# State-space stage of a streaming encoder: decay of the initial states and sums of squares on VectorE in place of Pool

## The chip, the core and the metric

The kernel runs on one core of a Trainium2 chip. The metric is the device time of one execution in microseconds (us). Five engines work side by side, each through its own instructions in order: TensorE (PE, with its weight loads as PEld), VectorE (DVE), ScalarE (ACT), Pool (GpSimd) and SyncE (SP), which here only starts transfers. TensorE writes into PSUM, in banks of 512 floats per partition; VectorE and ScalarE read them out. An instruction waits on semaphores for what it needs, and everything behind it on its engine waits too.

## The reference

One layer of a hybrid encoder for two groups of requests: a prompt of 1024 frames, and 8 requests of 16 frames with a past (caches of keys and values, of the convolution and of the state). After a modulated norm there is one input projection; branch A is chunked attention, branch B a state-space scan (Mamba-2 SSD); the two are gated, merged and projected. The change lies in branch B:

```python
def step(h, inp):                      # h: state per head, (64, 128)
    x, d, bk, ck = inp
    a_cs = jnp.cumsum(d * ag, axis=1)
    ...
    y_in = jnp.einsum('blsge,bsgep->blgep', cb[..., None] * decay, xdt)
    y_st = jnp.einsum('blgn,bgepn->blgep', ck, h) * jnp.exp(a_cs)[..., None]
    h_new = h * jnp.exp(a_cs[:, -1])[..., None, None] + jnp.einsum(...)
...
y = y * jax.nn.silu(z_ssd)
y = rms_norm(y.reshape(b, s, SSD_GROUPS, 512), ...)
```

For the 8 requests `h` starts from `state_ssm`: each new state is the initial state times its decay, plus a product over the 16 frames. The norm needs the sum of squares of `y` over a group of 512 channels, which are four pairs of heads of 128 channels.

## The kernel before

All 1152 tokens (1024 + 8 x 16) lie along the free axis, channels along the 128 partitions. The projections are float32 products in three parts: weights and activations are split into a high and a low half, and each output of 128 x 384 takes 8 x 3 matmuls (L384, L385, L387, the "dense" matmuls); the split of a weight block is L321 on ScalarE and L322 on VectorE. Outputs collect in PSUM tiles `d` (two banks) and `s` (one); small products use the tiles `g` out of a pool `psg` of four banks. `pg()` hands out a `g` tile, and its next user waits until the old one has been read.

The stages follow each other: attention over 8 units, then the state-space stage (about 860 to 1640 us of the span) over 16 pairs of heads in 4 groups, then the output projections.

In the state-space stage a pair `p` consists of three generators. `dense_gen` issues the dense matmuls of x (evicted by L1066 to L1070, then the convolution L1086 to L1096) and of z (L1255, L1256), and in ten pairs those of a merge gate (evicted by L1187, stored by L1188). `prelude` loads the decays, broadcast over the partitions (L1273, L1277), and the initial states (L1279), and makes the decay matrices (L1285, L1289 on ScalarE, L1291 on VectorE). `main` does the pair's own products:

- transposes of x (L1313), scaled by L1317; halves of the last rows for the requests' states (L1339, L1340) and their masked copies, four per pair, on Pool (L1347)
- the chunk states L1358 (`g` tiles), chained by L1363 and L1367; the last one is stored (L1372)
- the outputs within chunks L1385 (three `g` tiles), the initial states' part L1392, then L1398 on VectorE; the chunk states' part L1405, then L1410 and L1411
- the initial states times their decays, L1418 on Pool, 128 x 1024
- gating with z, L1419 on VectorE; y is stored (L1421), its square made on ScalarE (L1422)
- the requests' state products L1429 into two `g` tiles, two masked copies for each; each tile is added to the decayed states on VectorE (L1438); the result is stored (L1447)
- the squares are added up over the group's four pairs, L1444 on Pool, 128 x 1152 (the first pair's square is the start, so there are twelve additions)

After a group's fourth pair the sums go over the partitions (L766) and through a square root; the next group's transposes and products (L1216, L1222) share the same four banks.

The order of the work is not the order of the text. `run` steps the generators by a clock of estimated nanoseconds: a generator that yields a number has issued so much TensorE work, and `pause(t)` holds it until the clock has gone on by `t`. A scheduler then sorts the instructions by its own estimate of when they can start, so on each engine an instruction can move past others; `late(...)` keeps some in order. After a build the order on every engine is fixed.

Of the kernel before, what the change touches and what calls it, by code (L numbers as in the profile page):

```python
# [10 lines left out]
ALU = mybir.AluOpType  # L11

P = 128
# [3 lines left out]
NB = 8  # L17
# [4 lines left out]
HD = 64  # L22
# [89 lines left out]
def trunk_kernel(ctx: ExitStack, tc: tile.TileContext, h):  # L112
    nc = tc.nc
# [104 lines left out]
    def alloc(lay, tag, cols):  # L218
        if lay is L_Q:
            try:  # L220
                return alloc(L_QR, tag, cols)
            except NoSlot:
                pass
        if lay is L_SSD and tag == "H":
            try:
                return Buf(qarena, qarena.alloc(L_QS, "ada", cols), cols)
            except NoSlot:
                pass
        if lay is L_Q or lay is L_QS:
            return Buf(qarena, qarena.alloc(lay, tag, cols), cols)  # L230
        if lay is L_W3 or lay is L_VT or lay is L_VA:
            return Buf(varena, varena.alloc(lay, tag, cols), cols)
        if lay is L_H or lay is L_W or lay is L_WA or lay is L_QR or lay is L_ST:
            return Buf(rarena, rarena.alloc(lay, tag, cols), cols)
        if (lay is L_SSD or lay is L_HEAD or lay is L_TAIL) and tag == "T" or lay is L_HEAD and tag == "Y":
            if v_open[0]:
                try:
                    return alloc(L_VT, "T", cols)
                except NoSlot:
                    pass  # L240
        return Buf(arena, arena.alloc(lay, tag, cols), cols)
# [250 lines left out]
    sq = [alloc(L_START, "T", NT) for _ in range(2)]  # L492
# [211 lines left out]
    def until(t):  # L704
        while clock[0] < t:
            yield -1.0

    def pause(t):
        yield from until(clock[0] + t)
# [522 lines left out]
    def ssd(p):  # L1232
# [8 lines left out]
        s4 = decs.rearrange("p (b e) -> p b e", e=32)  # L1241
# [53 lines left out]
        def main():  # L1295
            yield from ready(lambda: "z" in st and "cbm" in grp[g] and "t" in dts and st["x"])
            x, tx = st["x"][0]
            z = st["z"]
            res = grp[g]
# [115 lines left out]
            stored(hst)  # L1415

            h4 = h0.ap.rearrange("p (b e d) -> p b e d", e=2, d=HD)
            nc.gpsimd.tensor_tensor(h4, h4, s4[:, :, 2 * p:2 * p + 2].unsqueeze(3).to_broadcast([P, NB, 2, HD]), ALU.mult)  # L1418
            nc.vector.scalar_tensor_tensor(x.ap, x.ap, 0.5, z.ap, ALU.mult, ALU.mult)  # L1419
            yield from pause(1800)  # L1420
            store(y_d[p], x.ap)  # L1421
            nc.scalar.activation(z.ap, x.ap, AF.Square)  # L1422
# [18 lines left out]
            if res["sq"] is None:  # L1441
                res["sq"] = z
            else:
                nc.gpsimd.tensor_tensor(res["sq"].ap, res["sq"].ap, z.ap, ALU.add)  # L1444
                z.free()
            yield from pause(1200)
            store(h["out_hs"][p], h0.ap)  # L1447
# [1 line left out]
            if p % PPG == PPG - 1:  # L1449
# [8 lines left out]
                if p == NPAIR - 1:  # L1458
                    dts["x"].free()

        return dense_gen(), [prelude()], [main()], 0.5


# [285 lines left out]
```

## Time and profile before

| | |
|---|---|
| time, median of 3 runs | 2037.41 us (2037.35 to 2038.08) |
| the profiled execution | 2043.03 us, span 2041.2 us |
| TensorE busy | 2014.5 us, 99% of the span |
| VectorE / ScalarE / Pool busy | 1163.9 / 766.0 / 405.9 us |
| granted TensorE clock, mean | 0.994 |
| TensorE's longest waits | 10.0 us at the start, 4.2 us in the state-space stage |
| L1418 on Pool | 16 times, median 1.91 us |
| L1444 on Pool | 12 times, median 2.67 us |

How to read the lines: the list of waits names who waited for what, with the total in us, the number of times and the longest. The chain gives start, duration and engine of the work that ended last. A timeline row gives start, duration, engine, line, operation, output and inputs, and in brackets the idle time before it and what ended it. A window row gives its bounds and length, then the busy time of PE, PEld, DVE, ACT and POOL with instruction counts, the granted clock (1.00 is full), the share of the DMA engines and GB/s. A row of groups ends with busy time and mean duration, then the idle time before the group. A row of one line gives the shortest, median and longest duration in ns.

### The profile page before, as it was taken

To read this page: it belongs to the slowest core of one execution; us is meant where nothing else is said; L and a number is where in the kernel's file an instruction comes from. 1 tells how busy PE (TensorE), PEld (TensorE's weight loads), DVE (VectorE), ACT (ScalarE), POOL (GpSimd) and SP (SyncE) were. 2 spreads that over 40 slices of the span, in tenths; PEclk is the share of its full clock that TensorE was granted. 3 is DMA by queue.
4 is the path that set the end of the run, shared out by engine and by line. 5 is a ranking of instruction groups with operands and counts; after the bars stand their busy time and mean duration, and the time that the engine had idled before them with its cause. 6 is when DMAs were issued, how large, how long until landed. Compare 5 with 4: busy or idle time off the path is not lost.

```text
span 2041.2 us, 35394 instructions
## 1 busy us (share of the span) xinstructions
PE 2014.5 (99%) x14223; PEld 1879.7 (92%) x14223; DVE 1163.9 (57%) x2424; ACT 766.0 (38%) x1560; POOL 405.9 (20%) x657
## 2 busy tenths in 40 slices
PE   7999999999999999999999999999999999999999
PEld 5888888888888888999999999999999999999999
DVE  6445454554554566456775677557764533777732
ACT  5344443443434444444534444345443311111210
POOL 0123121231212210123332234224323210000000
PEclk9999999999999999999999999999998999999999
DMA  7233232332323232333333433243325663331331
GB/s 311 88 103 104 72 127 76 127 101 95 110 86 127 68 102 84 103 123 120 121 99 111 124 109 121 93 126 128 120 89 191 251 224 103 126 100 54 100 118 62
DMA packets 81371, 239.63 MB, mean 117 GB/s; under 512 B 14316, under 2 KB 15352, under 8 KB 81208
## 3 DMA queue, kind: packets, MB, share of 16 engines
q1 hardware_dynamic: 72248, 208.73, 31.3%
q0 software_dynamic: 8960, 28.65, 3.6%
q8 instruction: 112, 1.84, 0.4%
q14 instruction: 51, 0.42, 0.1%
HBM read 193.39 MB, written 43.95 MB: 116 GB/s over the span
## 4 chain that ended last, share of the span: by engine, by line
PE 96%; DVE 2%; DMA 1%; ACT 1%; issue 0%; SPq 0%; DVEq 0%; ACTq 0%
PE d L384 13%; PE d L387 13%; PE d L385 13%; PE s L384 5%; PE d L440 5%; PE s L385 5%; PE d L438 5%; PE s L387 5%; PE d L439 5%; PE g L969 4%; PE g L908 3%; PE s L939 3%; PE g L1385 2%; PE g L1358 1%; PE g L1405 1%; PE g L1028 1%
## 5 line engine op out<-in xcount | busy, mean ns | idle before, releaser
L384 PE MATMUL d<-rarena 128*128 128x384 f32 x1536 | 527.8, 344 | 1.0 <-ACT rarena L321 1.0
L385 PE MATMUL d<-rarena 128*128 128x384 f32 x1536 | 518.3, 337 | 0.0
L387 PE MATMUL d<-rarena 128*128 128x384 f32 x1536 | 517.5, 337 | 0.2 <-DVE rarena L322 0.2
L384 PEld LDWEIGHTS d<-rarena 128*128 128x128 f32 x1536 | 289.7, 189 | 6.3 <-issue 3.8
L387 PEld LDWEIGHTS d<-rarena 128*128 128x128 f32 x1536 | 289.4, 188 | 3.0 <-issue 2.1
L385 PEld LDWEIGHTS d<-rarena 128*128 128x128 f32 x1536 | 290.0, 189 | 1.8 <-issue 1.5
L321 ACT ACTIVATE rarena<-arena 128x1024 fp32r<-128x1024 f32 x97 | 102.6, 1058 | 301.0 <-PE s L385 188.6
L384 PE MATMUL s<-rarena 128*128 128x384 f32 x624 | 213.6, 342 | 1.3 <-DVE arena L901 1.3
L385 PE MATMUL s<-rarena 128*128 128x384 f32 x624 | 209.7, 336 | 0.0
L387 PE MATMUL s<-rarena 128*128 128x384 f32 x624 | 209.5, 336 | 0.0
L438 PE MATMUL d<-va_att,rarena 128*128 128x384 f32 x576 | 200.1, 347 | 0.3 <-DVE arena L689 0.3
L440 PE MATMUL d<-va_att,rarena 128*128 128x384 f32 x576 | 199.4, 346 | 0.0
L439 PE MATMUL d<-va_att,rarena 128*128 128x384 f32 x576 | 198.0, 344 | 0.0
L322 DVE TENSOR_TENSOR rarena<-arena,rarena 128x1024 fp32r<-128x1024 f32 x97 | 125.9, 1298 | 94.3 <-ACT rarena L321 93.3
L901 DVE CUSTOM_DVE_ANT_0 arena<-s,arena 128x320 f32<-128x320 f32 (+5 forms) x208 | 99.5, 513 | 135.1 <-PE s L939 112.3
L896 ACT ACTIVATE arena<-arena 128x640 f32<-128x640 f32 (+3 forms) x144 | 101.2, 706 | 97.0 <-DVE arena L901 51.8
L384 PEld LDWEIGHTS s<-rarena 128*128 128x128 f32 x624 | 117.8, 189 | 3.4 <-issue 1.6
L385 PEld LDWEIGHTS s<-rarena 128*128 128x128 f32 x624 | 117.9, 189 | 0.4 <-issue 0.4
L387 PEld LDWEIGHTS s<-rarena 128*128 128x128 f32 x624 | 117.6, 188 | 0.0
L440 PEld LDWEIGHTS d<-va_att,rarena 128*128 128x128 f32 x576 | 108.3, 188 | 7.0 <-issue 6.3
L438 PEld LDWEIGHTS d<-va_att,rarena 128*128 128x128 f32 x576 | 108.4, 188 | 6.8 <-issue 5.6
L910 ACT ACTIVATE arena<-g 128x512 f32<-128x512 f32 (+3 forms) x144 | 71.0, 522 | 114.0 <-PE g L908 113.6
(332 smaller groups left out, 3358.7 us busy)
## 6 DMA issues: line engine op xcount, KB each, us to landing
arena<-in_wall_dram SPq DMA_DIRECT2D x88, 512.0 KB, 3.9
arena<-in_kc_dram SPq DMA_DIRECT2D x64, 256.0 KB, 3.0
arena<-in_vc_dram SPq DMA_DIRECT2D x64, 256.0 KB, 2.8
arena<-acs_d SPq DMA_DIRECT2D x20, 576.0 KB, 3.6
gate_d<-arena POOLq DMA_DIRECT2D x48, 192.0 KB, 2.2
y_d<-arena POOLq DMA_DIRECT2D x15, 576.0 KB, 3.4
arena<-y_d SPq DMA_DIRECT2D x15, 576.0 KB
arena<-in_wssd_dram SPq DMA_DIRECT2D x16, 512.0 KB, 3.5
```

Source lines behind the costliest of these rows:

```text
L321: keep(nc.scalar.activation(hi.r[:, c], b.ap, AF.Copy))
L322: keep(nc.vector.tensor_tensor(lo.r[:, c], b.ap, hi.ap[:, c], ALU.subtract))
L384: nc.tensor.matmul(ps, hi.r[:, wc], kh.r[:, tok], start=k == 0, stop=False)
L385: nc.tensor.matmul(ps, hi.r[:, wc], kl.r[:, tok], start=False, stop=False)
L387: nc.tensor.matmul(ps, lo.r[:, wc], kh.r[:, tok], start=False, stop=k == nk - 1)
L438: nc.tensor.matmul(ps, kh.r[:, tok], hi.r[:, wc], start=k == 0, stop=False)
L439: nc.tensor.matmul(ps, kh.r[:, tok], lo.r[:, wc], start=False, stop=False)
L440: nc.tensor.matmul(ps, kl.r[:, tok], hi.r[:, wc], start=False, stop=k == KT - 1)
L896: nc.scalar.activation(p, p, AF.Exp, bias=sm_[:, 4 + e:5 + e], scale=-1.0, accum_out=sm_[:, 6 + e:7 + e])
L901: late(nc.vector.tensor_tensor_reduce(p, ps, bap, -1.0, 3.0e38, ALU.add, ALU.min, least))
L910: nc.scalar.activation(pt.ap[:, j * P:(j + n) * P], ps[:, :n * P], AF.Copy)
L969: nc.tensor.matmul(ps[e * HD:e * HD + HD, :], v.ap[:, vc:vc + HD], pts[e].ap[:, j * P:(j + 1) * P], start=j == 0, stop=j == np_ - 1)
```

## The change

The product of the initial states with their decays goes from Pool to VectorE, and in the generator it stands behind the gating and a pause of 800. The addition of the squares goes from Pool to VectorE in its place. No instruction is added or taken away. All lines from L1418 on carry other numbers in the changed file: the gating is L1418, the product L1420, the store of y L1422, the square L1423, the state products L1430, the state addition L1439, the addition of squares L1445.

```diff
             h4 = h0.ap.rearrange("p (b e d) -> p b e d", e=2, d=HD)
-            nc.gpsimd.tensor_tensor(h4, h4, s4[:, :, 2 * p:2 * p + 2].unsqueeze(3).to_broadcast([P, NB, 2, HD]), ALU.mult)
             nc.vector.scalar_tensor_tensor(x.ap, x.ap, 0.5, z.ap, ALU.mult, ALU.mult)
+            yield from pause(800)
+            nc.vector.tensor_tensor(h4, h4, s4[:, :, 2 * p:2 * p + 2].unsqueeze(3).to_broadcast([P, NB, 2, HD]), ALU.mult)
             yield from pause(1800)
             store(y_d[p], x.ap)
             nc.scalar.activation(z.ap, x.ap, AF.Square)
...
             else:
-                nc.gpsimd.tensor_tensor(res["sq"].ap, res["sq"].ap, z.ap, ALU.add)
+                nc.vector.tensor_tensor(res["sq"].ap, res["sq"].ap, z.ap, ALU.add)
                 z.free()
```

## The prediction

> **What bounds the kernel now.** I read the page first, then the list of TensorE's waits, then the stage in windows, and last the chain and the timelines around the one long wait of the stage that the change touches.
>
> ```profile
> span 2041.2 us, 35394 instructions
> PE 2014.5 (99%) x14223; PEld 1879.7 (92%) x14223; DVE 1163.9 (57%) x2424; ACT 766.0 (38%) x1560; POOL 405.9 (20%) x657
> PE 96%; DVE 2%; DMA 1%; ACT 1%; issue 0%; SPq 0%; DVEq 0%; ACTq 0%
> ```
> ```profile
> PE g L503 <- DMA arena<-in_xT_dram: 10.0, 1, 10.0
> PE g L1385 <- DVE arena L1438: 4.2, 1, 4.2
> PE s L597 <- DVE rarena L584: 3.4, 4, 1.6
> ```
> ```profile
> 804.90:808.30 3.40, 1.82 (x16) 1.18 (x14) 3.40 (x12) 3.40 (x6) 0.92 (x3) 1.00 0.28 54
> 808.35:811.70 3.35, 3.35 (x11) 3.35 (x12) 3.35 (x5) 2.45 (x6) 0.00 (x0) 0.50 0.70 262
> 1532.20:1535.30 3.10, 0.00 (x0) 0.00 (x0) 3.10 (x1) 0.00 (x0) 2.35 (x1) 1.00 1.04 351
> 1535.40:1545.50 10.10, 9.12 (x71) 9.12 (x72) 8.00 (x26) 1.25 (x3) 3.09 (x3) 0.50 0.75 217
> 860.00:1640.00 780.00, 775.12 (x5515) 765.01 (x5514) 500.02 (x793) 328.38 (x654) 234.67 (x315) 0.99 0.39 130
> ```
>
> TensorE is busy 99% of the span and carries 96% of the chain. The change removes no matmul. So VectorE's and Pool's shares decide nothing by themselves: the time can move only where TensorE waits, or where its clock is cut. In the state-space stage (860 to 1640 us) VectorE is busy 500 of 780 us, Pool 235, TensorE 775. What TensorE lacks there is one place, its wait in L1385 for the second state addition L1438, in pair 14 (counted from 0). The chain through it:
>
> ```profile
> 1507.07 0.89 PE g L1358 x8
> 1508.13 0.17 PE s L385
> 1518.85 1.24 issue
> 1523.79 1.27 DVE arena L1291
> 1526.65 1.14 DVE va_ssd L1095
> 1527.78 0.20 DVE va_ssd L1096
> 1529.02 1.34 DVE arena L1419
> 1530.38 1.17 ACT arena L1422
> 1531.56 4.08 DVE rarena L322
> 1535.63 0.61 DVE arena L1438
> 1545.29 0.32 PE d L384
> 1545.83 0.18 PE d L387
> ```
> ```profile
> 1531.05 0.29 PE L1385 MATMUL g<-arena,va_ssd 128*64 128x128 f32 x1 [0.64 <-issue]
> 1531.87 0.27 PE L1385 MATMUL g<-va_ssd 128*64 128x128 f32 x1
> 1536.38 0.45 PE L1385 MATMUL g<-arena,va_ssd 128*64 128x128 f32 x1 [4.23 <-DVE arena L1438]
> ```
> ```profile
> 1531.25 0.73 POOL L1347 TENSOR_TENSOR rarena<-rarena,arena 128x256 fp32r<-128x256 f32 x1
> 1531.95 2.60 POOL L1444 TENSOR_TENSOR arena<-arena 128x1152 f32<-128x1152 f32 x1
> ```
>
> L1385 fills three PSUM tiles out of a pool of four, and its second tile takes the bank of the state product that L1438 adds up. TensorE idles 0.64 + 4.23 = 4.87 us. Then comes a part that a list of waits does not show: from 1535.4 to 1545.5 the granted clock is 0.50 (a 128x384 matmul advances by 0.32 us, afterwards by 0.18), so the 9.12 us of work in that window lose 9.12 / 2 = 4.6 us. This one place costs 4.87 + 4.6 = 9.4 us.
>
> **The change part by part.**
>
> ```profile
> L1418 POOL TENSOR_TENSOR qa_ssd<-qa_ssd,arena x8: 1902/1914/2030, 875.2 to 1540.5; 128x1024 f32<-128x1024 f32 x8
> L1444 POOL TENSOR_TENSOR arena<-arena x6: 2597/2673/2997, 1186.6 to 1622.3; 128x1152 f32<-128x1152 f32 x6
> L322 DVE TENSOR_TENSOR rarena<-arena,rarena x97: 1209/1222/4093, 20.6 to 2013.4; 128x1024 fp32r<-128x1024 f32 x97
> L1291 DVE TENSOR_TENSOR arena<-arena x13: 1345/1351/2474, 1077.7 to 1578.8; 128x1152 f32<-128x1152 f32 x13
> ```
>
> *What leaves Pool and comes to VectorE.* Sixteen products h0 x decay at 1.91 us and twelve additions of squares at 2.67 us leave Pool. No row shows them on VectorE. Its product of the same 1024 columns has a median of 1.22 us (L322), its product of 1152 columns 1.35 us (L1291); between nothing and Pool's own 1.91 and 2.67 I take these, being the same kind of instruction on the same engine. VectorE gains 16 x 1.22 + 12 x 1.35 = 35.7 us over the stage, 2.6 us in a pair with both. Where VectorE is not awaited this costs nothing: TensorE's dense matmuls cover it (between a pair's state products and the next pair's L1358 stand some 110 to 150 of them in most pairs, 19 to 26 us). Where that cover is gone, in pair 14, the 2.6 us are on the path and are in the sum below.
>
> *What VectorE no longer meets.* L322 at 1531.56 takes 4.08 us in place of 1.22. It began while Pool ran L1347, Pool's L1444 followed from 1531.95 to 1534.55, and L322 ended 1.1 us after that. Without L1444 on Pool 2.87 us of it go. [...]
>
> *The pause and the order.* The pause of 800 moves the planner's clock, and with it everything behind. In the built order nothing but that order changed from pair 1 on, and the product stands early, between L1410 and L1411, ahead of the gating (L1419, in the changed file L1418): the pause doesn't hold it back there. What matters is pair 14. In the built order of before 75 dense matmuls stand between the first L1358 of pair 13 and the second L1385 tile of pair 14, in the new one 81, with the same other matmuls. After the bank's last state product, before: 5 of L1358 and one tile of L1385 ahead of its reuse; now 10 dense, 8 of L1358 and that tile (the trace shows each L1358 and L1385 as two records). By row spacings the distance grows from 2.1 to 4.5 us. No other reuse of a bank in the stage is closer than 3.3 us now, and reuses that near stood elsewhere in the old order without a wait.
>
> *TensorE's side of pair 14.* From 1507.07 to the end of the first L1385 tile (1531.87 + 0.27) are 25.1 us, less 0.64 idle 24.4. Six more dense matmuls at 0.174 make 25.5. The second tile adds 0.9, and at 26.4 comes a gate's dense matmul whose bank waits for L1256.
>
> *VectorE's side.* L1438 ended at 1536.24, 29.2 us after 1507.07. In the new order L322 (4.08) and L1095 with L1096 (1.14 + 0.20) stand behind that addition, and the two moved instructions (1.22 + 1.35) before it: 29.2 - 4.08 - 1.34 + 2.57 = 26.3 us. Both L1291 now stand later, behind the gating, so the 1.24 us in which VectorE waited for the first one's exponentials can go too: 25.1 us. Against 25.5 TensorE waits 0 to 0.8 us. Then L322 (1.22) and L1256:
>
> ```profile
> L1256 DVE SCALAR_TENSOR_TENSOR arena<-arena,d 128x384 f32<-128x384 f32 x23 | 12.5, 548 | 3.3 <-ACT arena L1255 3.1
> ```
>
> 26.9 to 28.1 us, against 26.4: 0.5 to 1.7 us of waiting in all. I take 1.1.
>
> *The clock after a short wait.* The first two windows above show 1.58 us without a matmul, and then 3.35 us at clock 0.50: 1.7 us lost, against 4.6 behind the idle 4.23. The nearest case thus says 1.7; but the matmuls around that gap were small ones, here they are dense, so I charge half, 0.85. [...]
>
> *New waits in order.* The addition of squares now waits on VectorE for ScalarE's Square, with the second L1438 queued behind it and TensorE behind that. Square takes 1.17 us from the end of the gating, and two L1291 (2.6 us) stand between: covered in pair 14. On Pool the masked copies (L1347) and the stores of y and of the state move up; SP's loads of h0 wait for those stores and can only come sooner. That is taken as nothing, since TensorE waits for none of them before.
>
> **Sum.** -9.4 + 1.1 + 0.85 = -7.4 us. The profiled execution took 2043.0 us, its span 2041.2 with 1.8 around it; it would become 2035.6. The median of the runs is 2037.4, 5.6 below the profiled one; I carry the same difference over: **2030.0 us**.
>
> **The rivals.** About 0.2% (4.1 us) is what a measurement of this kernel can tell from no change: 2033.3 and 2041.5 are the bounds.
>
> *The same wait again.* TensorE's gate matmul waits for L1256, that for L1255, and that for the store of the pair's y:
>
> ```profile
> ACT arena L1255 <- DMA y_d<-arena: 4.4, 1, 4.4
> 1530.65 0.58 POOL L1421 DMA_DIRECT2D y_d<-arena  x1 [1.51 <-PE g L1358]
> ```
>
> The store issued at 1530.65 let L1255 go at 1536.11, 5.4 us on. In the new order the gating ends some 19.4 us after the first L1358 (23.3 - 2.6 - 1.3 - 1.2 + 1.2), so the store lands at about 25.4 and L1256 ends at 26.4, in time. Were it to land 5 us later, the 4.9 us of waiting and the half clock would be back: 2037.4.
>
> *The wait is smaller without the profiler.* The runs are 5.6 us shorter than the profiled execution; if part of that is this very wait, less is there to win. With half of it gone, 4.7 - 2.0 = 2.7 us: 2034.7. The narrow spread of the runs (0.7 us) speaks neither for nor against.
>
> *Slower: the group boundaries.* At the starts of groups 1 to 3 (pairs 3, 7, 11) transposes and products for the next group share the four banks with the state products. Reuse distances there are 3.7 to 5.1 us, and the built order now puts the addition of squares, waiting in order for Square, right before the evictions:
>
> ```profile
> 1229.45 1.22 DVE L1095 SCALAR_TENSOR_TENSOR arena<-arena 128x1024 f32<-128x1024 f32 x1
> 1232.99 2.85 DVE L322 TENSOR_TENSOR rarena<-arena,rarena 128x1024 fp32r<-128x1024 f32 x1 [0.93 <-ACT rarena L321]
> 1235.76 0.68 DVE L1224 TENSOR_TENSOR arena<-g,arena 128x512 f32<-128x512 f32 x1
> ```
>
> Against it: L322 took 2.85 there and nothing waited, and those 1.6 us of collision go. It decides from the point where the eviction comes later than its reuse: if the moved 2.6 us came on top in full at each boundary with 1.7 us of clock, 3 x 4.3 = 12.9 are lost, and with the 7.4 won the kernel takes 2042.9.
>
> **How the numbers follow.** The forecast has 0.66; its own range runs from 0.5 us of waiting and a full clock (gain 8.9, 2028.5) to a gain of 4.1 (2033.3). The same wait 0.12 and the smaller wait 0.10 fall within 0.2%; the boundaries 0.12. The range for 8 in 10 takes in the first three: 2028.0 to 2038.0.
>
> **What would show it.** Right: no wait of TensorE for L1439 above 2 us, the clock of the stage at 1.00 but for at most one short cut, L322 in pair 14 at 1.2 us, the new VectorE rows at 1.2 and 1.35 us. Wrong: a wait of 3 us or more at L1385 or at the matmul behind it, a new half clock at a group boundary (about 1030, 1230 or 1420 us), or VectorE's rows near Pool's 1.9 and 2.7 us.

## The result, and the profile after

The changed kernel takes 2031.47 us (median of 7 runs, 2029.64 to 2035.69), beside 2037.41 us for the kernel before (7 runs, 2035.56 to 2038.15). The medians differ by 5.9 us. The ratio of the runs is 0.9968, with a 95% interval of 0.9958 to 0.9977; it is taken over the runs and is not quite the quotient of the two medians, here and in the tables below. The forecast was 2030.0 us.

The profiled execution took 2029.88 us. The lines of its page that answer to those shown of before:

```profile
span 2028.1 us, 35366 instructions
PE 2007.2 (99%) x14223; PEld 1871.0 (92%) x14223; DVE 1166.3 (58%) x2452; ACT 766.3 (38%) x1560; POOL 336.3 (17%) x629
PE 98%; DVE 1%; DMA 0%; ACT 0%; issue 0%; SPq 0%; ACTq 0%; DVEq 0%
```

TensorE's list of waits, first the wait at the start, then the whole list for the state-space stage:

```profile
PE g L503 <- DMA arena<-in_xT_dram: 8.7, 1, 8.7
...
PE d L384 <- DVE arena L1256: 0.4, 1, 0.4
```

The wait at L1385 is gone. What is left of it is 0.4 us, at the gate's dense matmul behind the second tile. The chain through this place shows who is last there now (start, duration, engine):

```profile
1523.31 0.85 DVE arena L1445
1524.16 0.73 issue
1524.89 0.68 DVE arena L1439
1525.56 1.13 DVE rarena L322
1526.69 0.48 DVE arena L1256
1527.21 0.44 PE d L384
```

VectorE is still the last to come, with the moved addition L1445 in its row, but L322 takes its 1.1 to 1.2 us and not 4.08. The windows behind it (bounds, length, busy time of TensorE first, the granted clock as third number from the end) show a full clock:

```profile
1524.45:1527.88 3.43, 3.04 (x41) 2.68 (x40) 3.43 (x6) 0.92 (x3) 1.58 (x2) 1.00 0.47 122
1527.88:1531.30 3.42, 3.42 (x21) 3.42 (x20) 3.42 (x9) 0.00 (x0) 0.00 (x0) 1.00 0.97 320
```

**Where the 13 us between the two profiled executions come from.** The median moved by 5.9 us, these two executions differ by 13.1. Both issue 14,223 matmuls, in the same order up to the state-space stage and with some of them moved inside it, so their times can be compared matmul by matmul (start of the n-th matmul of the trace, us):

| matmul | before | after | difference | grown by | what lies in between |
|---|---|---|---|---|---|
| 1st | 10.00 | 8.71 | -1.29 | -1.29 | the first input's DMA |
| 5,000th | 679.12 | 676.21 | -2.91 | -1.62 | start: 6.8 us of half clock before, 3.4 after |
| 5,500th | 748.33 | 743.86 | -4.46 | -1.55 | half clock at 733 us, before only |
| 6,000th | 816.59 | 810.58 | -6.02 | -1.55 | half clock at 808 us, before only |
| 11,000th | 1511.81 | 1506.32 | -5.50 | +0.52 | pairs 0 to 12, pair 13 up to L1392 |
| end of the last | 2037.40 | 2024.00 | -13.40 | -7.90 | the rest of pair 13, pair 14, and all behind it |

Only the last two rows can be the change's doing, since the kernels are the same up to the state-space stage. The pairs up to pair 13 lose half a microsecond, and from there on 7.9 are gained: 8.6 up to the 11,800th matmul, at the end of the stage (1634.12 and 1620.07 us), of which 0.7 is lost again behind it, without a new wait of TensorE. The 6.0 us ahead of the stage are differences between executions, which the last section comes back to.

### The profile page after: what moved, and what is told of

The parts are those of the page before. It is cut to its first block, busy times and chain, and to the rows that moved or that the text cites. A ratio compares the mean times of both kernels' runs of the same rounds, so it can differ in the third digit from the quotient of the medians.

```text
span 2028.1 us, 35366 instructions
## 1 busy us (share of the span) xinstructions
PE 2007.2 (99%) x14223; PEld 1871.0 (92%) x14223; DVE 1166.3 (58%) x2452; ACT 766.3 (38%) x1560; POOL 336.3 (17%) x629
## 3 DMA queue, kind: packets, MB, share of 16 engines
q8 instruction: 112, 1.84, 0.4%
## 4 chain that ended last, share of the span: by engine, by line
PE 98%; DVE 1%; DMA 0%; ACT 0%; issue 0%; SPq 0%; ACTq 0%; DVEq 0%
PE d L384 14%; PE d L387 13%; PE d L385 13%; PE s L384 5%; PE s L385 5%; PE s L387 5%; PE d L440 5%; PE d L438 5%; PE d L439 5%; PE g L969 4%; PE g L908 3%; PE s L939 3%; PE g L1385 2%; PE g L1358 1%; PE g L1405 1%; PE g L1028 1%
## 5 line engine op out<-in xcount | busy, mean ns | idle before, releaser
L322 DVE TENSOR_TENSOR rarena<-arena,rarena 128x1024 fp32r<-128x1024 f32 x97 | 119.4, 1231 | 93.7 <-ACT rarena L321 93.6
```

Source lines behind the costliest of these rows:

```text
L322: keep(nc.vector.tensor_tensor(lo.r[:, c], b.ap, hi.ap[:, c], ALU.subtract))
```

## The experiments

Two causes stood together in the chain of before, and the change removes both: the order (the bank of the second L1385 tile is reused after 2.1 us of matmuls, with the change after 4.5), which the pause sets, and the collision of L322 with the addition of squares on Pool (4.08 us beside it, 1.22 at the median). Theory *order* says the pause does it, theory *collision* the engines. I took them apart, and gauge each kernel by three things: TensorE's waits in pair 14, the half clock behind them, and the time from the 11,000th matmul to the end of the last, against the 525.59 us of before. That last number leaves out what happens ahead of the stage. All three are read from one profiled execution of each kernel; the waits repeat from the change's first execution to its second, but whether a half clock follows a wait can differ between executions (last section).

### One part at a time

Additions of squares alone on VectorE, no pause:

```diff
-                nc.gpsimd.tensor_tensor(res["sq"].ap, res["sq"].ap, z.ap, ALU.add)
+                nc.vector.tensor_tensor(res["sq"].ap, res["sq"].ap, z.ap, ALU.add)
```

> Only the additions of squares (L1444) go to VectorE; the products stay on Pool ahead of the gating and there is no pause, and the built order of TensorE is that of before. Theory order (the pause's new order takes the wait away, not the engines): TensorE still waits in pair 14 at the second L1385 tile for the state addition, 3 us or more, and the time is 2035 to 2037.5. Theory collision (Pool's addition of squares holds up VectorE's L322 by 2.87 us, and that is the wait): L322 takes 1.2 us in pair 14, the wait falls from 4.2 to about 1.4 us, the half clock behind it shrinks or goes, and the time is 2030 to 2033.

Both operations on VectorE, no pause:

```diff
-            nc.gpsimd.tensor_tensor(h4, h4, ..., ALU.mult)
+            nc.vector.tensor_tensor(h4, h4, ..., ALU.mult)
             nc.vector.scalar_tensor_tensor(x.ap, x.ap, 0.5, z.ap, ALU.mult, ALU.mult)
...
-                nc.gpsimd.tensor_tensor(res["sq"].ap, res["sq"].ap, z.ap, ALU.add)
+                nc.vector.tensor_tensor(res["sq"].ap, res["sq"].ap, z.ap, ALU.add)
```

> Both operations go to VectorE where they stood, without the pause; the built order of TensorE is close to that of before (the bank of the second L1385 tile is reused after about 2 us in place of 4.5). VectorE's work up to the second state addition sums to 24.1 us, without the collision, plus 1.2 us of waiting for exponentials: 25.3, against some 24.4 of TensorE. Theory order: a wait at L1385 of 1 to 3 us stays, with or without a stretch of half clock, and the time is 2032 to 2036. Theory collision: the wait is 1 us or less and the time within 1.5 us of the changed kernel's 2031.5.

The pause alone, both operations on Pool:

```diff
             nc.vector.scalar_tensor_tensor(x.ap, x.ap, 0.5, z.ap, ALU.mult, ALU.mult)
+            yield from pause(800)
             yield from pause(1800)
```

> Only the pause of 800 behind the gating is added; product and addition of squares stay on Pool. The built order of TensorE becomes that of the changed kernel. Theory order: no wait at L1385 above 0.5 us, no half clock in 1500 to 1560 us, time 2029.5 to 2032.5, as the changed kernel (2031.5). Theory collision: Pool's addition still meets a VectorE instruction in pair 14, a wait of 2 to 4 us stays, and the time is 2034 to 2037.5.

The pause and the product, the additions on Pool:

```diff
-            nc.gpsimd.tensor_tensor(h4, h4, ..., ALU.mult)
             nc.vector.scalar_tensor_tensor(x.ap, x.ap, 0.5, z.ap, ALU.mult, ALU.mult)
+            yield from pause(800)
+            nc.vector.tensor_tensor(h4, h4, ..., ALU.mult)
```

> The pause and the product on VectorE behind it, the additions of squares stay on Pool. The built order is that of the changed kernel. Theory order: as the changed kernel, no wait above 0.8 us at L1385 or behind it, 2029.5 to 2032.5. Theory collision: L322 in pair 14 meets Pool's L1445 again and takes 2.5 to 4.1 us in place of 1.2; as it now stands ahead of L1256, TensorE's dense matmul behind the second L1385 tile waits 2 to 3.5 us, and the time is 2033 to 2037.

TensorE's waits in the state-space stage of these four, in the order above (additions alone; both without the pause; pause alone; pause and product):

```profile
PE g L1385 <- DVE arena L1438: 1.7, 1, 1.7
PE g L1385 <- DVE arena L1398: 1.2, 1, 1.2
PE g L1385 <- issue: 0.6, 1, 0.6
```
```profile
PE g L1385 <- DVE arena L1398: 1.2, 1, 1.2
PE g L1385 <- DVE arena L1438: 1.1, 1, 1.1
PE g L1385 <- issue: 0.6, 1, 0.6
```
```profile
PE d L384 <- DVE arena L1256: 2.1, 1, 2.1
```
```profile
PE d L384 <- DVE arena L1256: 3.8, 1, 3.8
PE g L1216 <- DVE arena L1224: 0.9, 1, 0.9
```

| kernel | waits in pair 14, us | half clock behind, us | 11,000th matmul to end, against before | median of runs, us | ratio, 95% interval |
|---|---|---|---|---|---|
| before | 4.87 | 10.24 | | 2038.02 | |
| additions | 3.5 | 6.83 | -2.69 | 2034.61 | 0.9984 (0.9972 to 0.9995) |
| additions and products | 3.0 | none | -5.51 | 2034.82 | 0.9986 (0.9976 to 0.9997) |
| pause | 2.1 | 3.41 | -4.97 | 2033.13 | 0.9969 (0.9957 to 0.9982) |
| pause and products | 3.8 | 3.41 | -3.45 | 2035.63 | 0.9982 (0.9973 to 0.9992) |
| the change (beside 2037.41) | 0.4 | none | -7.90 | 2031.47 | 0.9968 (0.9958 to 0.9977) |

Neither theory holds alone. Of the 4.87 us of waiting the pause alone removes 2.8 and the two moves alone 1.9; that makes 4.7, and the change, which does both, removes 4.5. So each theory missed somewhere. With the additions alone L322 takes 1.52 us in pair 14, and the wait at the second L1385 tile falls to 1.7 us: collision expected about 1.4, order 3 and more. That 3.5 us are left in all comes from a wait that neither expected, of the third L1385 tile for L1398, 1.2 us; the median of 2034.61 lies between the two ranges. With both moves and no pause 3.0 us of waiting stay, as order expects; with the pause alone 2.1 us, as collision expects. These statements rest on the waits in the traces. By the medians the pause alone cannot be told from the whole change: the intervals of the two ratios overlap nearly in full.

What still delays VectorE with the pause alone are two collisions. Rows of the timelines of VectorE and Pool in order of time (start, duration):

```profile
1507.94 3.54 DVE L1089 SCALAR_TENSOR_TENSOR arena<-arena 128x1176 f32<-128x1176 f32 x1
1508.31 1.93 POOL L1418 TENSOR_TENSOR arena<-arena 128x1024 f32<-128x1024 f32 x1
1512.33 1.43 DVE L1089 SCALAR_TENSOR_TENSOR arena<-arena 128x1176 f32<-128x1176 f32 x1
1523.05 3.62 POOL L1445 TENSOR_TENSOR arena<-arena,va_ssd 128x1152 f32<-128x1152 f32 x1 [1.72 <-ACT va_ssd L1423]
1524.21 2.92 DVE L1340 TENSOR_TENSOR rarena<-arena,rarena 64x128 fp32r<-64x128 f32 x2
```

L1089 takes 3.54 us beside Pool's product, and 1.43 in the row of its next execution; the two L1340 take 2.92 beside Pool's addition, where the changed kernel's trace has 0.60. Together they cost VectorE 4.4 us in this one pair. By the durations the two rows nearly go one behind the other: Pool's 1.93 and L1089's own 1.43 make 3.36 us, and L1089 took 3.54. The starts in the record do not show it: L1089 stands there 0.37 us ahead of Pool's product, and yet ends 1.24 us after it.

With the product on VectorE and the addition left on Pool it got worse than with the pause alone, by a way I had not expected. L322 met nothing (1.21 us). But VectorE waited in order for a buffer:

```profile
1530.06 2.72 POOL L1445 TENSOR_TENSOR arena<-arena,va_ssd 128x1152 f32<-128x1152 f32 x1 [3.60 <-ACT va_ssd L1423]
1530.31 0.69 DVE L1439 TENSOR_TENSOR arena<-arena,g 128x512 f32<-128x512 f32 x1
1532.82 1.62 DVE L1095 SCALAR_TENSOR_TENSOR va_ssd<-arena 128x1024 f32<-128x1024 f32 x1 [1.82 <-POOL arena L1445]
```

L1095, the convolution of the next pair's x, writes into a `va_ssd` buffer, and L1445 reads `z` out of one and then frees it. Pool ends at 1532.78, VectorE starts L1095 at 1532.82, and L1256 is queued behind that. VectorE's built order plays a part in it too: in the changed kernel L1095 stands behind the L1256 of this place, here ahead of it. So the addition on Pool can cost in two ways, by collision (2.32 us at the two L1340 with the pause alone) or by freeing its buffer late (1.82 us of idle VectorE ahead of L1095 here).

### Where it lies, and how much room there is

The changed kernel with the pauses merged behind the gating and the product ahead of it:

```diff
+            nc.vector.tensor_tensor(h4, h4, ..., ALU.mult)
             nc.vector.scalar_tensor_tensor(x.ap, x.ap, 0.5, z.ap, ALU.mult, ALU.mult)
-            yield from pause(800)
-            nc.vector.tensor_tensor(h4, h4, ..., ALU.mult)
-            yield from pause(1800)
+            yield from pause(2600)
```

> The changed kernel with both operations on VectorE, but the product stands ahead of the gating and the two pauses (800, then 1800) are one of 2600 behind it, so that the planner's clock runs on by as much in all. The built order is then close to that of before: the second L1385 tile of pair 14 reuses its bank after 2.3 us (changed kernel: 4.5), and VectorE's work up to the second state addition sums to 22.9 us as in the changed kernel. Theory order and engines together (each takes a part of the wait): a wait of 1 to 3 us at L1385, 2032 to 2036. Rival, that the pause's length is what counts and not where it stands: no wait above 0.5 us in pair 14, 2029.5 to 2032.5.

Each product twice (a repeat of the line in the changed kernel, so that the decay is applied twice):

```diff
             nc.vector.tensor_tensor(h4, h4, ..., ALU.mult)
+            nc.vector.tensor_tensor(h4, h4, ..., ALU.mult)
```

> The changed kernel, with each product of initial state and decay done twice on VectorE (16 x 1.22 us more in the stage). In pair 14 the work up to the gate's L1256 grows from 24.5 to 26.7 us in the built order. Theory (TensorE waits there for what VectorE is late, everything else is covered): the wait in pair 14 grows from 0.4 to 2 to 3 us, with or without a half clock of 3.4 us behind it, the other pairs cost nothing, 2032 to 2035.5. Rival, that VectorE has slack there too: no wait above 0.8 us, 2029.5 to 2032.5.

The change in all pairs but pair 13, and the change in pair 13 alone. The first as a diff to the changed kernel; the second has the conditions the other way round:

```diff
+            if p == 13:
+                nc.gpsimd.tensor_tensor(h4, h4, ..., ALU.mult)
             nc.vector.scalar_tensor_tensor(x.ap, x.ap, 0.5, z.ap, ALU.mult, ALU.mult)
-            yield from pause(800)
-            nc.vector.tensor_tensor(h4, h4, ..., ALU.mult)
+            if p != 13:
+                yield from pause(800)
+                nc.vector.tensor_tensor(h4, h4, ..., ALU.mult)
...
-                nc.vector.tensor_tensor(res["sq"].ap, res["sq"].ap, z.ap, ALU.add)
+                (nc.vector if p != 13 else nc.gpsimd).tensor_tensor(res["sq"].ap, res["sq"].ap, z.ap, ALU.add)
```

> The change in every pair but pair 13 (counted from 0), which keeps product and addition of squares on Pool and has no pause; the additions and matmuls of pair 13 lie beside the place in pair 14 where TensorE waited. The built order of TensorE in pair 14 is near that of the changed kernel (no reuse of a bank below 3.3 us). Theory (all of the effect lies at this one place, and Pool's addition beside it holds VectorE up by 2 to 4 us): TensorE waits 1.5 to 4 us in pair 14, 2032.5 to 2036.5. Rival (the effect is the sum over the pairs): as the changed kernel to within 0.5 us of waiting, 2029.5 to 2032.5.

> The change in pair 13 alone; all other pairs as before. The built order stays that of before up to pair 13, and the second L1385 tile of pair 14 reuses its bank after 2.3 us. Theory order and engines together: the addition is off Pool at the one place that counts, so the wait falls from 4.9 us to 1 to 3 us but does not go, 2032 to 2036. Rival (engines alone, at this place): below 0.8 us of waiting, 2029.5 to 2032.5.

TensorE's waits in pair 14, in the order merged pause, product twice, all but pair 13, pair 13 alone:

```profile
PE g L1385 <- DVE arena L1438: 1.2, 1, 1.2
PE d L384 <- DVE arena L1256: 0.9, 1, 0.9
```
```profile
PE g L1385 <- DVE arena L1398: 2.1, 1, 2.1
```
```profile
PE g L1385 <- DVE arena L1442: 3.3, 1, 3.3
PE d L384 <- DVE arena L1256: 0.2, 1, 0.2
```
```profile
PE g L1385 <- DVE arena L1442: 1.2, 1, 1.2
PE d L384 <- DVE arena L1256: 0.9, 1, 0.9
PE g L1385 <- DVE va_ssd L1291: 0.8, 1, 0.8
```

| kernel | waits in pair 14, us | half clock behind, us | 11,000th matmul to end, against before | median of runs, us | ratio, 95% interval |
|---|---|---|---|---|---|
| before | 4.87 | 10.24 | | 2037.99 | |
| merged pause | 2.1 | none | -6.37 | 2035.26 | 0.9987 (0.9977 to 0.9997) |
| product twice | 2.1 | 3.41 | -4.57 | 2035.52 | 0.9989 (0.9979 to 1.0000) |
| all pairs but 13 | 3.5 | 6.83 | -1.96 | 2038.13 | 0.9999 (0.9989 to 1.0008) |
| pair 13 alone | 2.8 | none | -5.44 | 2033.72 | 0.9988 (0.9977 to 0.9999) |

- *Merged pause.* The waits fell into the range of the theory, not to the rival's 0.5: where the pause stands counts, since it decides the order, and not its length alone.
- *Product twice.* The waits are in the forecast range of 2 to 3 us. The built order asks 2.2 us more of VectorE ahead of L1256, and the wait grew by 1.7 (0.4 to 2.1). It now shows one matmul group earlier, at the third L1385 tile, which waits for L1398. So VectorE has next to no slack at this place. In the other pairs the further products left no wait of TensorE at all.
- *All but pair 13.* The wait of 3.5 us is as expected, but the gain of the median is gone (I had expected 2032.5 to 2036.5): fifteen pairs changed bring nothing that the median shows if pair 13 keeps product and addition on Pool and has no pause; in the trace they bring 1.96 of the 7.90 us. The Pool addition of pair 13 stretches L1096 in the trace from 0.28 to 2.70 us, and L1089 takes 3.54 beside the product. As in the change 81 dense matmuls stand ahead of the second L1385 tile, so it is VectorE that comes late here, and not the bank that is reused sooner.
- *Pair 13 alone.* It takes the waits from 4.9 to 2.8 us, as the theory says, and no further: its built order has the bank reused after 2.3 us.

### What the product on VectorE costs there, and once more the change

The pause and the additions, the products on Pool:

```diff
             nc.vector.scalar_tensor_tensor(x.ap, x.ap, 0.5, z.ap, ALU.mult, ALU.mult)
+            yield from pause(800)
             yield from pause(1800)
...
-                nc.gpsimd.tensor_tensor(res["sq"].ap, res["sq"].ap, z.ap, ALU.add)
+                nc.vector.tensor_tensor(res["sq"].ap, res["sq"].ap, z.ap, ALU.add)
```

> The pause and the additions of squares on VectorE; the products stay on Pool ahead of the gating. In pair 14 VectorE's work up to the gate's L1256 sums to 22.3 us in the built order (changed kernel 24.5, where 0.4 us of waiting were left), and Pool's addition is gone. Theory (the wait is the order's part plus Pool's addition's part, the product adds only work on VectorE): no wait of TensorE at all in pair 14, no half clock there, and the time is that of the changed kernel or up to 0.5 us below, 2029 to 2032. Rival (taking the product off Pool matters too, by its collisions of 1.9 us): a wait of 1 to 2 us stays in pair 14, 2032 to 2034.

> The changed kernel once more, beside the kernel with pause and additions alone. If the half clocks at about 733 and 808 us depend on where those places fall in a fixed row of 3.41 us stretches, which shifts from execution to execution, then they are in some of its runs and not in others, at about 3 us for the two: times near 2030 and near 2033, median 2030 to 2033. If they belonged to the kernel before alone, all runs would be near 2030.

With pause and additions 2030.79 us (5 runs, 2030.12 to 2034.52; ratio 0.9962, 0.9948 to 0.9976), the changed kernel again 2031.57 (8 runs, 2029.77 to 2035.78; 0.9971, 0.9961 to 0.9981), before 2037.62. The two cannot be told apart. The eight runs of the change do not fall into two heaps as cleanly as expected, but their time goes with the mean clock: 2029.8 to 2031.1 us at 0.999 (four runs), 2032.1 and 2032.4 at 0.998, 2033.6 at 0.997, 2035.8 at 0.996. From the 11,000th matmul to the end they take 517.94 and 517.71 us, 7.6 and 7.9 less than before; the first execution of the change had 517.69.

The list of waits of pause and additions has one line, and the timeline shows why it is not empty though VectorE has 2.2 us less to do in the built order (L1089 beside Pool's product, and its undisturbed next execution):

```profile
PE d L384 <- DVE arena L1256: 0.4, 1, 0.4
```
```profile
1511.68 3.54 DVE L1089 SCALAR_TENSOR_TENSOR arena<-arena 128x1176 f32<-128x1176 f32 x1
1512.04 1.93 POOL L1418 TENSOR_TENSOR arena<-arena 128x1024 f32<-128x1024 f32 x1
1516.06 1.43 DVE L1089 SCALAR_TENSOR_TENSOR arena<-arena 128x1176 f32<-128x1176 f32 x1
```

I had expected no wait; it is 0.4. The product on Pool holds L1089 up by 2.1 us, which is what was saved. Left on Pool the product delays VectorE, moved to VectorE it costs its 1.2 us. So of the three parts the pause and the addition carry the gain, and the product's move is worth nothing that these runs can tell. No version tried here is measurably faster than the change.

## Why the prediction was right

**The place.** The gain of the trace lies in pair 14 and the end of pair 13, as forecast. The change everywhere but in pair 13 leaves 3.5 us of the waiting and no gain of the median; the change in pair 13 alone brings 5.44 of the 7.90 us.

**The size.** The sum said -7.4 us against the profiled execution; from the 11,000th matmul on it is -7.90. Its terms:

- *The wait.* 4.87 us became 0.39, where I took 1.1 out of 0.5 to 1.7. VectorE's side was worked out as 25.1 to 26.3 us from the first L1358 of pair 13 to the end of the second state addition. In the trace they are at 1500.35 and 1525.57: 25.2. That the 1.24 us of waiting for the exponentials go was the right end of the range. TensorE reaches the gate's matmul at 1526.82, 26.5 us behind the same start, where I had 26.4.
- *The half clock left over.* I charged 0.85 us, half of the nearest case; there is none. Half of it could not come: in these traces such a stretch comes whole (3.41, 6.83 or 10.24 us in the tables) or not at all (below).
- *The half clock won.* I took 4.6 us for the 10.24 us at clock 0.50, half of the 9.12 us of work. That is too much. By the rows a dense matmul advances by 0.32 us at half clock and by 0.174 at full, 1.84 times and not twice, which makes 4.2. And the kernel with both moves and no pause had no half clock, nearly the same order and 1.89 us less waiting, and gained 5.51, so the cut is worth some 3.6, an estimate from these two traces. Three smaller errors thus cancelled in part: 0.7 in the wait and 0.85 of clock that the change did better, 0.9 of the old clock that it did worse. That the sum came within half a microsecond is in so far luck.

**Durations of the moved instructions.** Forecast 1.22 and 1.35 us. Rows of the changed kernel (shortest, median, longest in ns):

```profile
L1420 DVE TENSOR_TENSOR arena<-arena x8: 1216/1220/1221, 918.7 to 1598.7; 128x1024 f32<-128x1024 f32 x8
L1445 DVE TENSOR_TENSOR arena<-arena x4: 1346/1356/1359, 1182.2 to 1610.2; 128x1152 f32<-128x1152 f32 x4
L322 DVE TENSOR_TENSOR rarena<-arena,rarena x97: 1210/1224/1637, 19.4 to 2000.0; 128x1024 fp32r<-128x1024 f32 x97
```

The addition in pair 14 itself took 1.66 us, beside a masked copy (L1347) on Pool.

What I did not see is the other side of that account. I wrote that VectorE gains 35.7 us, which are hidden. Its busy time went from 1163.9 to 1166.3 us, by 2.4. The 28 instructions are 19.5 + 17.5 us by their rows, so the busy time of the other VectorE instructions fell by 34.6 us (by the sum of their rows, which overlap a little, by 29.6). Line by line, L1411 fell by 13.5 us, L322 by 6.5 (125.9 to 119.4 over its 97 executions), L1291 by 4.9, L1096 by 4.3. L1411 in the state-space stage before and after, the larger of its groups (busy time and mean duration behind the bar):

```profile
L1411 DVE TENSOR_TENSOR arena<-arena 128x128 f32<-128x128 f32 (+2 forms) x27 | 20.5, 763 | 0.8
L1411 DVE TENSOR_TENSOR arena<-arena 128x128 f32<-128x128 f32 (+2 forms) x27 | 13.6, 509 | 0.3
```

In this stage of before 39 VectorE rows are over 0.2 us longer than the lower quartile of their own line and shape, together by some 35 us. Every one of them overlaps a computing row of Pool, as only 226 of all 792 rows do; eleven are L1411 beside the product L1418. In the changed kernel 23 such rows are left, some 8 us. That the overlap caused all of the lengthening is inferred from this. I had credited one collision, the 2.87 us of L322 in pair 14.

**From the profile to the median.** I carried the 5.6 us between profiled execution and median over, and this is the step that worked least well. The median fell by 5.9 us (4.7 to 8.6 by the interval), the place itself by 7.9 in each of two traces of the change. The interval holds both the forecast's 7.4 and the 7.9. But the granted clocks of the runs say that the place gives less in other executions. The profiled execution of before had 26.6 us at half clock in all and a mean clock of 0.994; of the 72 runs of before taken beside the experiments 7 are at 0.994, 38 at 0.996 and 7 at 0.999. In these last the 10.24 us at half clock behind the wait cannot have been there, for they alone bring the mean down by 0.0025, to 0.9975. These seven take 2034.3 to 2035.9 us, median 2035.07; the change's seven runs at 0.999 have a median of 2030.74. That is 4.3 us less, about the wait alone (4.5), though not all of them ran on one chip. The wait thus seems to be there in the other executions too, and the half clock behind it only in some; the sum took it from an execution that had more half clock than most. That the forecast of the median still came within 1.5 us is partly luck.

**The rivals.** *The same wait again*: the store of y was in time, L1255 ended at 1524.82, ahead of the end of the state addition. *Group boundaries*: no wait there in the changed kernel; in the kernel with pause and product alone it did appear, 0.9 us at L1216, with 1.2 us of time lost by the count of matmuls. The mechanism exists, at some quarter of the 4.3 us that I gave it. *Smaller without the profiler*: borne out in part, for the half clock, as said; for the wait itself no run shows it.

## What to carry to other kernels

Where one engine is busy 99% of the time, find its one wait and follow it into the instruction that was last: a duration of three times the usual one with another engine's row beside it, as L322's 4.08 us in place of 1.22 beside L1444 on Pool, did not show in the list of waits here. An operation that is moved off the other engine can cost its new engine next to nothing, if it had been paying for it before: here VectorE took over 37.0 us of work and its busy time grew by 2.4; look at its total before and after. And a wait on a shared buffer has two sides, the order of who needs it and the speed of who frees it: try the two apart, since each may give only half (here 2.8 and 1.9 of the 4.87 us of waiting).

## What the runs showed of the hardware

**In these traces the half clock comes in stretches of 3.41 us.** In the trace of before the granted clock changes at 23.24, 30.07, 733.21, 736.62, 808.30, 811.72, 1535.34, 1545.58 and 2040.52 us of the span, each a whole multiple of 3.413 us behind the first (2, 208, 209, 230, 231, 443, 446 and 591 of them); in the changed kernel's at 23.29, 26.70 and 2026.91 (1 and 587). The two rows lie 0.05 us apart, while the same work, the 6,000th matmul, stands at 816.59 and at 810.58 us: where the row lies against the work differs from execution to execution. At about 805 us all kernels do the same work with the same idle gap of 1.3 us, and a shorter one of 0.3 us ahead of it (1.31 and 0.27 in the trace of before). Six of the twelve traces have half clock behind this gap, the other six a full clock. In before, in both moves without the pause and in pause and additions, the stretch that holds the gap has 1.83 us of TensorE work (the shorter gap lies in it too), and half clock follows; in the changed kernel's first execution it has 2.11 us, and a full clock follows. Two such stretches of the changed kernel, to be held against the first two windows shown of before (1.82 us of work, then 0.50):

```profile
801.48:804.90 3.42, 2.11 (x17) 1.71 (x14) 3.42 (x8) 3.13 (x4) 0.78 (x3) 1.00 0.57 175
804.90:808.31 3.41, 3.41 (x22) 3.41 (x21) 3.41 (x8) 1.74 (x4) 0.00 (x0) 1.00 0.61 167
```

Pair 14 shows the same. First both moves without the pause, 3.0 us of waiting spread over three stretches, of which this is the emptiest, then the pause alone, 2.1 us in one:

```profile
1530.69:1534.10 3.41, 1.55 (x25) 1.10 (x20) 3.41 (x6) 0.00 (x0) 0.53 (x1) 1.00 1.10 346
1534.10:1537.51 3.41, 2.93 (x48) 2.93 (x49) 3.41 (x11) 1.26 (x3) 0.00 (x0) 1.00 0.85 284
```
```profile
1525.45:1528.86 3.41, 1.32 (x14) 1.08 (x14) 3.35 (x6) 0.82 (x3) 2.97 (x4) 1.00 0.19 58
1528.86:1532.28 3.42, 3.42 (x12) 3.42 (x11) 3.42 (x8) 0.00 (x0) 0.00 (x0) 0.51 1.06 306
```

Of the stretches of pair 14 that ran at full clock and could be laid out on their trace's own row, the six with 0.21 to 1.47 us of work were followed by half clock, and none with 1.54 or more; of those at half clock, two of before, with 2.38 and 3.42 us, were followed by another one. The busy time alone does not decide it: a stretch at 61 us of the changed kernel with 1.78 us was followed by a full clock, and the half clock of before at 733 us has no gap ahead of it at all. There matmul records fill the whole stretch, more than half of them small (of 32, 18 are L1114, 64x32, in 2.1 us):

```profile
729.81:733.22 3.41, 3.41 (x32) 3.17 (x30) 1.14 (x2) 3.10 (x7) 0.25 (x2) 1.00 0.43 178
```

What decides it, these runs don't tell.

This is why my half charge of 0.85 us could not come true as such, why the same work at 733 and at 808 us costs 1.55 us more in one execution than in the next, and, by the mean clocks of the runs, a good part of why runs of one kernel lie 3 to 9 us apart: with additions and products on VectorE without the pause, six of twelve runs lie at 2032.4 to 2033.9 us with a mean clock of 0.999 to 1.000, three at 2039.6 to 2040.4 with 0.995.
